# First norm's weights moved to the transposed rows, and the opening's queues written out by hand

## The chip, the cores and the metric

The kernel runs on one core of one Trainium2 chip. The metric is the device time of one execution in microseconds (us). Three executions of the kernel before took 1943.76, 1944.37 and 1944.44 us; the median is 1944.37 us.

## The reference

One layer is computed (DEPTH is 1) on 1024 tokens of width 1024 in float32: a feed-forward half step, an attention step and a second feed-forward half step. The change lies wholly in the first feed-forward step, and in what stands ahead of its first products:

```python
def rms_norm(x, gain):
    y = x * rsqrt(mean(x * x, axis=-1) + 1e-6)
    return y * gain

def swiglu(xn, w_in, w_out):          # w_in: 1024 x 5632, w_out: 2816 x 1024
    gate, up = split(xn @ w_in, 2)
    return (silu(gate) * up) @ w_out

x = x + 0.5 * swiglu(rms_norm(x, n1), wi1, wo1)      # n1 is g1 in the kernel
x = x + stick_breaking_attention(rms_norm(x, mix_norm), ...)
x = x + 0.5 * swiglu(rms_norm(x, n2), wi2, wo2)
```

## The kernel before, in words

**Three matmuls for one.** Each float32 operand is split into a high part, rounded to the matmul's own format by a copy on ACT, and a low part, which is the operand less its high part (`split`, L195: ACT at L197, the subtraction on DVE or POOL at L199). A product is then high by high, high by low and low by high, added up in PSUM (`mm3`, L347 to L349).

**The first feed-forward step.** The 2816 hidden columns are taken in 11 pairs of blocks of 128 (q = 0 to 10), gate and up. The rows of x are eight tiles of 128 tokens; the tokens of tiles 4 to 7 are the half T0, those of tiles 0 to 3 the half T1. Each row tile is normed (`norm`, L282), transposed on TensorE against an identity matrix (`turned`, L302, the transposes at L326, four into one PSUM bank), and split into `xh` and `xl`, which hold all of x transposed, eight blocks k of 128 features by 1024 tokens. Pair q = 0 is computed directly (`first_pair`, L433): four keys, (0,0), (1,0), (0,1) and (1,1), each a block of 128 hidden columns of gate (second number 0) or up (1); for each key and each half of the tokens 24 matmuls (8 blocks k by three). `FIRST[0]` (L64) gives the order of these, with the column ranges: 256 wide for as long as rows come in by pairs, 512 wide otherwise. The later pairs (`ffn_in`, L469) go by seven products instead of eight (`seven`, L532), which need sums of the quarters of x as well. These sums are the four tiles `tl`, which `turned` builds from the same PSUM banks (`mixes`, L310: copies on ACT, subtractions on DVE and one on POOL), and which `ffn_in` splits (L492) while the first pair runs on TensorE.

**The norm.** The sum of squares of a row tile is taken by halves of 512 features: one half on ACT (Square with a sum, L269), the other on DVE (L263). POOL adds the halves (L279), adds epsilon (L221) and raises to the power -0.5 (L222). DVE then scales the row by that rate and by the norm's weights in one instruction (L295). The weights vary along the row there, so they must stand in all 128 partitions: one row of 4 KB is loaded on ACT's queue (L230), spread over the partitions by two matmuls with a row of ones into two `ka` banks (L236), read from there for the first two rows and then copied to SBUF (L241), which frees the two banks.

**The opening.** SP's queue loads row tiles 4 and 5, the weights of gate for q = 0 (two transfers of 512 KB, runs of 1 KB), row tiles 6 and 7, the weights of up, row tiles 0 to 3 (`load_x`, `stream`, L748 to L752). TensorE runs 14 idle matmuls on zeros, before and between the first transposes (`WARM`, L70; L723). The first key runs on `mm3_late` (L352), which puts the matmuls with low parts last. Rows 6 and 7, then 0 and 1, then 2 and 3 are turned ahead of the steps (1,0), (1,2) and (4,0) of `FIRST[0]` (`turn_rows`, L733, and the table `at`, L775).

**What sets the order.** Each engine works through one queue in order. The program's scheduler fills the queues by priority, which is roughly the order of the program text; `following(mark)` puts an instruction behind the marked one on the same engine, without a wait for its end. Only some of the opening's instructions carry such a mark before.

Of the kernel before, what the change touches and what calls it, by code (L numbers as in the profile page):

```python
# [69 lines left out]
WARM = ((4, 3), (2, 1), (2, 2))  # L70
# [44 lines left out]
def macaron_kernel(ctx, tc, x, g1, w1_in, w1_out, gm, w_qkv, gq, gk, w_o, g2, w2_in, w2_out, out):  # L115
# [68 lines left out]
    above = cpool.tile([P, 96], F32, name="above")  # L184
# [10 lines left out]
    def split(raw, hi, lo, engine=None, after=(None, None)):  # L195
        with following(after[0]):
            first = act.activation(hi, raw, AF.Copy).ins  # L197
        with following(after[1]):
            return first, (engine or dve).tensor_tensor(lo, raw, hi.bitcast(F32), op=ALU.subtract).ins  # L199
# [17 lines left out]
    def root(pool, ss, inv_n):  # L217

        n = ss.shape[-1]
        a, y = (pool.tile([P, n], F32, name=f"rs_{i}", bufs=b) for i, b in (("a", 4), ("y", 2)))  # L220
        pool_e.tensor_scalar(a, ss, inv_n, EPS, op0=ALU.mult, op1=ALU.add)  # L221
        marks["root"] = pool_e.tensor_tensor(y, a, power.to_broadcast([P, n]), op=ALU.pow).ins  # L222
        return y

    HALVES = [slice(c * NHALF, (c + 1) * NHALF) for c in range(2)]

    def spread_gain(pl, g, ones):

        t = pl["xs"].tile([P, D], F32, name="gain", bufs=1)
        act.dma_start(t[0:1], g)  # L230
        spread = [bank("ka") for _ in HALVES]

        def put():
            for to, c in zip(spread, HALVES):
                with following(marks["warm"]):
                    marks["warm"] = pe.matmul(to, ones, t[0:1, c], start=True, stop=True).ins  # L236

        def keep(after):
            for src, c in zip(spread, HALVES):
                with following(after):  # L240
                    act.activation(t[:, c], src, AF.Copy)  # L241
            return [t[:, c] for c in HALVES]

        return spread, put, keep
# [10 lines left out]
    def squares(pl, row, tbs, ss, halves=(0, 1), shared=None, after=None):  # L255

        for i, tb in enumerate(tbs):
            for h in halves:
                to = ss[:, i, h : h + 1]
                if shared is not None and h:  # L260
                    x_ = row(tb, h)
                    with following(after and after[1]):
                        marks["squared"] = dve.scalar_tensor_tensor(  # L263
                            out=shared(i), in0=x_, scalar=1.0, in1=x_, op0=ALU.mult, op1=ALU.mult, accum_out=to
                        ).ins
                    continue
                junk = pl["hs"].tile([P, NHALF], F32, name="hs", bufs=1)
                with following(after and after[0]):
                    act.activation(junk, row(tb, h), AF.Square, accum_out=to)  # L269

    def rates(pl, row, tbs, ss=None, pooled=False, shared=None, after=None):

        n = len(tbs)
        if ss is None:
            ss = pl["xs"].tile([P, n, 2], F32, name="ss")
            squares(pl, row, tbs, ss, shared=shared, after=after)
        st = pl["xs"].tile([P, n], F32, name="st")
        with following(marks.get("root") if pooled else None):
            (pool_e if pooled else dve).tensor_tensor(st, ss[:, :, 0], ss[:, :, 1], op=ALU.add)  # L279
        return root(pl["xs"], st, 1.0 / D) if pooled else rsqrt(pl["xs"], st, 1.0 / D)  # L280

    def norm(pl, row, tbs, gain, ss=None, r=None, behind=None, pooled=False, shared=False, after=None):  # L282
# [4 lines left out]
        if r is None:  # L287
            to = [pl["xs"].tile([P, D], F32, name="xs") for _ in tbs] if shared else None
# [993 lines left out]
```

## Time and profile before

| | |
|---|---|
| median of 3 runs | 1944.37 us |
| the profiled execution's own time | 1945.78 us |
| its span, first to last instruction | 1943.9 us |
| granted TensorE clock, mean | 0.999 |
| TensorE (PE) busy | 1911.3 us, 98% of the span |
| VectorE (DVE), ScalarE (ACT), GpSimd (POOL) busy | 64%, 51%, 57% |
| first matmul of the first key (L360) starts at | 15.69 us |
| first matmul of pair q = 1 (L347, `ka`, 512 wide) starts at | 73.17 us |

The span is one execution on the chip. PE is TensorE's matmuls, PEld its weight loads, DVE is VectorE, ACT is ScalarE, POOL is GpSimd, SP the engine that issues most transfers. In a row of the timeline stand the start from the beginning of the span, the length, the engine, the line of the kernel, the operation, output <- inputs, the shape, the number of instructions merged, and in brackets the idle time ahead of it with what ended that. In a row of groups stand the count, the busy time in us, the mean of one in ns, and the idle time ahead. In a row of windows stand, for each engine, the busy time and the number of instructions, then the granted clock, the share of the DMA engines and the rate in GB/s.

### The profile page before, as it was taken

To read this page: it belongs to the slowest core of one execution; us is meant where nothing else is said; L and a number is where in the kernel's file an instruction comes from. 1 tells how busy PE (TensorE), PEld (TensorE's weight loads), DVE (VectorE), ACT (ScalarE), POOL (GpSimd) and SP (SyncE) were. 2 spreads that over 40 slices of the span, in tenths; PEclk is the share of its full clock that TensorE was granted. 3 is DMA by queue.
4 is the path that set the end of the run, shared out by engine and by line. 5 is a ranking of instruction groups with operands and counts; after the bars stand their busy time and mean duration, and the time that the engine had idled before them with its cause. 6 is when DMAs were issued, how large, how long until landed. Compare 5 with 4: busy or idle time off the path is not lost.

```text
span 1943.9 us, 26741 instructions
## 1 busy us (share of the span) xinstructions
PE 1911.3 (98%) x9410; PEld 1627.5 (84%) x9410; DVE 1246.6 (64%) x1711; ACT 984.0 (51%) x1796; POOL 1106.9 (57%) x993
## 2 busy tenths in 40 slices
PE   8999999999999999999999999999999999999999
PEld 7878888888888898898989897788888888888887
DVE  6855545544775757878787788477555545548545
ACT  5433343344335467777787877344433443343332
POOL 4566666755455746656655665114667666654554
PEclk9999999999999999999999999999999999999999
DMA  5233232337997411011011135521323232369983
GB/s 196 72 106 120 98 103 88 128 106 268 345 321 259 138 33 43 29 46 47 28 39 44 60 110 173 175 74 45 130 87 125 92 103 95 124 206 345 326 274 142
DMA packets 168361, 259.71 MB, mean 134 GB/s; under 512 B 11553, under 2 KB 81185, under 8 KB 168226
## 3 DMA queue, kind: packets, MB, share of 16 engines
q1 hardware_dynamic: 168224, 258.00, 39.1%
q8 instruction: 74, 1.21, 0.3%
q14 instruction: 61, 0.50, 0.1%
q10 hardware_dynamic: 2, 0.00, 0.0%
HBM read 197.66 MB, written 60.29 MB: 133 GB/s over the span
## 4 chain that ended last, share of the span: by engine, by line
PE 82%; DVE 9%; ACT 3%; POOL 2%; issue 2%; DMA 1%; SPq 0%; ACTq 0%; DVEq 0%; POOLq 0%
PE ka L347 6%; PE ka L348 6%; PE ka L349 6%; PE kc L347 4%; PE kc L348 4%; PE kc L349 4%; PE bq L347 4%; PE kb L347 4%; PE kb L348 4%; PE kb L349 4%; PE bq L348 4%; PE bq L349 3%; PE ma L349 3%; PE ma L348 3%; PE ma L347 3%; PE mb L348 3%
## 5 line engine op out<-in xcount | busy, mean ns | idle before, releaser
L199 POOL TENSOR_TENSOR rp<-raw,rp 128x1024 fp32r<-128x1024 f32 x84 | 209.0, 2493 | 173.0 <-ACT rp L197 157.7
L199 POOL TENSOR_TENSOR u<-sf,u 128x512 fp32r<-128x512 f32 x160 | 227.2, 1422 | 137.2 <-ACT u L197 137.2
L199 POOL TENSOR_TENSOR u<-raw,u 128x512 fp32r<-128x512 f32 x135 | 198.0, 1471 | 159.5 <-ACT u L197 158.5
L988 POOL TENSOR_TENSOR w<-w,om 128x512 f32<-128x512 f32 (+4 forms) x128 | 141.0, 1105 | 114.9 <-DVE om L981 88.6
L197 ACT ACTIVATE u<-sf 128x512 fp32r<-128x512 f32 x160 | 100.9, 631 | 204.3 <-PE kb L348 87.1
L485 DVE TENSOR_TENSOR h<-h 128x512 f32<-128x512 f32 x110 | 135.4, 1234 | 85.9 <-POOL h L589 85.1
L197 ACT ACTIVATE rp<-rh 128x1024 fp32r<-128x1024 f32 (+1 forms) x78 | 76.6, 985 | 202.1 <-issue 73.8
L347 PE MATMUL bq<-wqh,xh 128*128 128x384 f32 x512 | 174.7, 341 | 0.0
L349 PE MATMUL bq<-wqh,xl 128*128 128x384 f32 x512 | 172.2, 336 | 0.0
L348 PE MATMUL bq<-wql,xh 128*128 128x384 f32 x512 | 172.1, 336 | 0.0
L197 ACT ACTIVATE u<-raw 128x512 fp32r<-128x512 f32 x136 | 85.1, 632 | 152.4 <-PE ka L348 100.1
L611 DVE TENSOR_TENSOR raw<-raw 128x1024 f32<-128x1024 f32 (+1 forms) x60 | 91.6, 1529 | 104.6 <-DMA raw<-w_out 94.9
L348 PE MATMUL ka<-xl,u 128*128 128x512 f32 (+1 forms) x408 | 153.8, 377 | 2.8 <-DVE xl L199 2.8
L347 PE MATMUL ka<-xh,u 128*128 128x512 f32 (+1 forms) x408 | 153.8, 377 | 2.0 <-ACT s L537 1.7
L349 PE MATMUL ka<-xh,u 128*128 128x512 f32 (+1 forms) x408 | 153.5, 376 | 0.0
L349 PE MATMUL ma<-rp 128*128 128x512 f32 x352 | 137.1, 389 | 0.6 <-DVE rp L199 0.6
L347 PE MATMUL ma<-rp 128*128 128x512 f32 x352 | 137.0, 389 | 0.0
L348 PE MATMUL ma<-rp 128*128 128x512 f32 x352 | 136.9, 389 | 0.0
L589 POOL TENSOR_TENSOR h<-h,g 128x512 f32<-128x512 f32 x80 | 113.0, 1413 | 35.8 <-DVE h L541 34.0
L979 ACT ACTIVATE w<-bz,f 128x512 f32<-128x512 f32 (+2 forms) x192 | 112.5, 586 | 40.1 <-PE bz L975 39.1
L514 DVE TENSOR_TENSOR sf<-raw 128x512 f32<-128x512 f32 x80 | 78.2, 978 | 78.0 <-POOL u L199 78.0
L199 DVE TENSOR_TENSOR rp<-rh,rp 128x1024 fp32r<-128x1024 f32 (+1 forms) x70 | 109.6, 1583 | 24.6 <-ACT rp L197 20.0
(292 smaller groups left out, 5481.1 us busy)
## 6 DMA issues: line engine op xcount, KB each, us to landing
raw<-w_out SPq DMA_DIRECT2D x120, 512.0 KB, 5.5
raw<-w_in SPq DMA_DIRECT2D x88, 512.0 KB, 3.6
k<-h SPq DMA_DIRECT2D x154, 256.0 KB, 2.0
rh<-k SPq DMA_DIRECT2D x64, 512.0 KB, 5.9
raw_qkv<-w_qkv SPq DMA_DIRECT2D x64, 192.0 KB, 2.9
x_keep<-x SPq DMA_DIRECT2D x32, 256.0 KB, 3.7
x<-x_keep SPq DMA_DIRECT2D x32, 256.0 KB, 5.3
raw<-w_out SPq DMA_DIRECT2D x24, 256.0 KB, 3.5
```

Source lines behind the costliest of these rows:

```text
L197: first = act.activation(hi, raw, AF.Copy).ins
L199: return first, (engine or dve).tensor_tensor(lo, raw, hi.bitcast(F32), op=ALU.subtract).ins
L347: pe.matmul(dst, ah, bh, start=start and i == 0, stop=False, skip_group_check=onto)
L348: pe.matmul(dst, ah, bl, start=False, stop=False, skip_group_check=onto)
L349: last = pe.matmul(dst, al, bh, start=False, stop=stop and i == n - 1, skip_group_check=onto)
L485: dve.tensor_tensor(src, hb[of[0]], hb[of[1]], op=getattr(ALU, of[2]))
L514: dve.tensor_tensor(f[n], x, y, op=op)
L589: pool_e.tensor_tensor(h, h, gs[k], op=ALU.mult)
L611: dve.tensor_tensor(w[0], w[0], w[1], op=getattr(ALU, W_OF[m][2]))
L979: act.activation(to, z, AF.Sigmoid, scale=state["f", half][:, sign, tb % 4, hd : hd + 1])
L988: pool_e.tensor_tensor(wt[:, c1 : c0 + n], wt[:, c1 : c0 + n], om[:, c1 - 1 : c0 + n - 1], op=ALU.mult)
```

## The change

The norm's weights come in as 128 x 8 (`g1_sb`: feature block k in column k), so that after the transpose they are one number per partition. DVE scales a row by its rate alone, from SBUF to SBUF; the weights are applied where the transposed rows leave PSUM: by ACT as a scale with the high part, by DVE as a scale in the same instruction that subtracts the high part (`less`). The spread by matmuls, its two banks and its copies are gone.

Rows are turned in blocks: 4 and 5 (256 columns for each k), 6 and 7, then all four of 0 to 3, features 0 to 511 ahead of the last key of T0, features 512 to 1023 ahead of T1. So T1 runs 512 wide throughout. The copies of tiles 4 to 7 into `tl` are no longer made by ACT from PSUM, but by POOL as high plus low part (`whole_x`, two instructions of 4 x 256 for each pair of rows).

The first transfer of weights goes in pieces of 128 columns (runs of 512 bytes), so that both halves of the first key come ahead of the second key. The 14 idle matmuls become 13, all ahead of the first transposes. The power function is run once on a constant before it is needed. Nearly every instruction of the opening on ACT, DVE and POOL goes through `go`, which puts it behind the one before it on its engine in program order; so do the transposes and the first key on TensorE. The first work of pair q = 1 is put behind the last of these on each engine (`marks["open"]`).

```diff
 FIRST = (
-    ((0, 0, 256, (0, 1, 2)), (0, 256, 256, (0, 1, 2)), (0, 0, 512, (3,)),
-     (1, 0, 256, (0, 1)), (1, 256, 256, (0, 1)), (1, 0, 512, (2, 3))),
+    ((0, 0, 256, (0, 1, 2)), (0, 256, 256, (0, 1, 2)), (0, 0, 512, (3,)), (1, 0, 512, (0, 1, 2, 3))),
...
-WARM = ((4, 3), (2, 1), (2, 2))
+IDLE = 13
...
+    def go(engine, emit):
+
+        with following(marks.get(engine)):
+            marks[engine] = emit().ins
...
+    def mm3_late(dst, pairs, late):
+
+        n = len(pairs)
+        steps = []
+        for i in range(n + late):
+            if i < n:
+                steps.append((i, 0, 0))
+            if 0 < i <= n:
+                steps.append((i - 1, 0, 1))
+            if i >= late:
+                steps.append((i - late, 1, 0))
+        for i, (k, a, b) in enumerate(steps):
+            go("pe", lambda: pe.matmul(dst, pairs[k][0][a], pairs[k][1][b], start=i == 0, stop=i == len(steps) - 1))
...
-            with sooner(SOON if q == 1 else 0):
+            with sooner(SOON if q == 1 else 0), ExitStack() as held:
+                for mark in marks.pop("open", ()):
+                    held.enter_context(tc.issue_after(mark))
                 us = prepare(stream(pl, w_in, q, 0))
...
+                def square(tb, h, engine="act"):
+                    if tb not in xs:
+                        xs[tb] = pl["xs"].tile([P, D], F32, name="xs", bufs=4)
...
+                def scale(tb, h):
+                    go("dve", lambda: dve.tensor_scalar(
+                        xs[tb][:, HALVES[h]], rows_of[tb][:, HALVES[h]], r[:, tb : tb + 1], None, op0=ALU.mult
+                    ))
...
+                def high_x(tps, tbs):
+                    c = slice(tbs[0] * P, (tbs[-1] + 1) * P)
+                    for k, tp in tps.items():
+                        go("act", lambda: act.activation(xh[:, k, c], tp, AF.Copy, scale=g1_sb[:, k : k + 1]))
+
+                def less(out, tp, k, of):
+                    go("dve", lambda: dve.scalar_tensor_tensor(
+                        out=out, in0=tp, scalar=g1_sb[:, k : k + 1], in1=of, op0=ALU.mult, op1=ALU.subtract
+                    ))
...
+                def whole_x(tbs):
+                    c, q = slice(tbs[0] * P, (tbs[-1] + 1) * P), slice(tbs[0] % 4 * P, (tbs[-1] % 4 + 1) * P)
+                    for d, t in ((0, tl[0]), (1, tl[3])):
+                        go("pool", lambda: pool_e.tensor_tensor(
+                            t[:, :, q], xh[:, 4 * d : 4 * d + 4, c].bitcast(F32),
+                            xl[:, 4 * d : 4 * d + 4, c].bitcast(F32), op=ALU.add,
+                        ))
...
-                ahead = [stream(pr, w1_in, 0, 0)]
+                ahead = [stream(pr, w1_in, 0, 0, 2)]
...
+                for d in range(2):
+                    low(0, 1, d, "dve")
+                    for h in range(2):
+                        scale(6 + d, h)
+                behind = xs[7][:, D - 1 :]
+                for d in range(2):
+                    high(1, 1, d)
+                for d in range(2):
+                    low(1, 1, d, behind=None if d else behind)
+                square(0, 0)
+                square(0, 1)
+                square(1, 0)
+                square(1, 1, "dve")
+                rate(0, 2)
+                whole_x((4, 5))
+
+                def second_half():
+                    tps = turn_x((6, 7), range(KD))
+                    high_x(tps, (6, 7))
+                    low_x(tps, (6, 7))
+                    for tb in (2, 3):
+                        square(tb, 0)
+                        square(tb, 1, "dve")
+                    rate(2, 2)
+                    whole_x((6, 7))
+                    for tb in range(4):
+                        for h in range(2):
+                            scale(tb, h)
+                    marks["open"] = [marks[e] for e in ("act", "dve", "pool")]
+
+                def first_rows(d):
+                    tps = turn_x(range(4), range(4 * d, 4 * d + 4))
+                    high_x(tps, range(4))
+                    if d == 0:
+                        for k, tp in tps.items():
+                            go("act", lambda: act.activation(tl[2][:, k], tp, AF.Copy, scale=g1_sb[:, k : k + 1]))
+                    low_x(tps, range(4))
+                    for k, tp in tps.items():
+                        t1, t2, t3, t4 = (t[:, k % 4] for t in tl)
+                        if d == 0:
+                            less(t1, tp, k, t1)
+                        else:
+                            less(t3, tp, k, t3)
+                            less(t2, tp, k, t1)
+                            go("pool", lambda: pool_e.tensor_tensor(t4, t4, t2, op=ALU.subtract))
+
+                turns = {(1, 0): second_half, (2, 3): partial(first_rows, 0), (3, 0): partial(first_rows, 1)}
+                hb = first_pair(pa | pr, us, turns, FIRST[0], True)
```

`turn_x` transposes the given row tiles, feature block by feature block; `low_x` calls `less` for each block; `high` and `low` make the two parts of a block of weights; `rate` makes the rates of one or two row tiles on POOL; `square` takes half a row's sum of squares on ACT or DVE. The order of ACT's, DVE's and POOL's instructions is that of these calls.

More of the change, by code (lines that the diff above doesn't have):

```diff
@@ L193, in following, with split @@
         return tc.issue_after(mark) if mark is not None else nullcontext()
[L195 to L199, printed above, removed]
+    def split(raw, hi, lo, engine=None):
+        first = act.activation(hi, raw, AF.Copy).ins
+        return first, (engine or dve).tensor_tensor(lo, raw, hi.bitcast(F32), op=ALU.subtract).ins
     def rsqrt(pool, ss, inv_n, y=None):
@@ L221, in root @@
         pool_e.tensor_scalar(a, ss, inv_n, EPS, op0=ALU.mult, op1=ALU.add)
-        marks["root"] = pool_e.tensor_tensor(y, a, power.to_broadcast([P, n]), op=ALU.pow).ins
+        pool_e.tensor_tensor(y, a, power.to_broadcast([P, n]), op=ALU.pow)
         return y
     HALVES = [slice(c * NHALF, (c + 1) * NHALF) for c in range(2)]
[L227 to L244, printed above, removed]
     def load_gain(pl, g):
@@ L253, in rows, with squares, rates @@
         return slice(tb * P, (tb + 1) * P)
-    def squares(pl, row, tbs, ss, halves=(0, 1), shared=None, after=None):
+    def squares(pl, row, tbs, ss, halves=(0, 1)):
         for i, tb in enumerate(tbs):
             for h in halves:
[L259 to L266, printed above, removed]
                 junk = pl["hs"].tile([P, NHALF], F32, name="hs", bufs=1)
-                with following(after and after[0]):
-                    act.activation(junk, row(tb, h), AF.Square, accum_out=to)
-    def rates(pl, row, tbs, ss=None, pooled=False, shared=None, after=None):
+                act.activation(junk, row(tb, h), AF.Square, accum_out=ss[:, i, h : h + 1])
+    def rates(pl, row, tbs, ss=None, pooled=False):
         n = len(tbs)
@@ L454, in first_pair @@
                 ]
-                marks["key"] = (mm3_late if early and (n, i) == (0, 0) else mm3)(
-                    ps[t][key][:, c0 : c0 + width], pairs, after=marks.get("key") if early else None
-                )
+                to = ps[t][key][:, c0 : c0 + width]
+                if early:
+                    mm3_late(to, pairs, 4)
+                else:
+                    mm3(to, pairs)
             left[t] -= len(ks)
@@ L718, in macaron_kernel @@
+                go("pool", lambda: pool_e.tensor_tensor(r[:, :1], r[:, :1], power, op=ALU.pow))
                 idle = bank("kc")
-                def warm(n):
-                    for _ in range(n):
-                        with following(marks.get("warm")):
-                            marks["warm"] = pe.matmul(idle, zeros[:, :P], zeros, start=True, stop=True).ins
-                def normed(tbs, shared=False, after=None, behind=None):
-                    pending.extend(
-                        norm(
-                            pl, lambda tb, h: rows_of[tb][:, HALVES[h]], tbs, gain,
-                            pooled=True, shared=shared, after=after, behind=behind,
-                        )
-                    )
@@ L733, in turn_rows @@
-                def turn_rows(tbs):
-                    while pending:
-                        pending.pop(0)("kb", tl, after=marks["key"])
-                    if tbs:
-                        normed(tbs, behind=marks["turned"][1])
-                def weight(j, part, d, *args, **kwargs):
-                    us.setdefault((j, part), []).append(
-                        unit(pa | pr, columns(ahead[part][d], j), *args, **kwargs)
-                    )
-                warm(WARM[0][0])
-                gain, put_gain, keep_gain = spread_gain(pl, g1, ones)
@@ new lines, in macaron_kernel @@
+                for d in range(2):
+                    high(0, 0, d)
+                high(1, 0, 0, "dve")
+                tps = turn_x((4, 5), range(KD))
+                for d in range(2):
+                    low(0, 0, d, behind=None if d else behind)
+                high_x(tps, (4, 5))
+                low_x(tps, (4, 5))
+                high(1, 0, 1)
+                for d in range(2):
+                    low(1, 0, d)
+                for tb in (6, 7):
+                    square(tb, 0)
+                    square(tb, 1, "dve")
+                    rate(tb)
```

179 lines of the change are left out of this document (97 added, 82 removed).

## The prediction

> **What bounds the kernel now.** I read the page first, then TensorE's time in three stretches.
>
> ```profile
> span 1943.9 us, 26741 instructions
> PE 1911.3 (98%) x9410; PEld 1627.5 (84%) x9410; DVE 1246.6 (64%) x1711; ACT 984.0 (51%) x1796; POOL 1106.9 (57%) x993
> ```
> ```profile
> 0.00:73.17 73.17, 65.56 (x394) 0.98 0.39 134
> ...
> 140.00:1943.90 1803.90, 1780.54 (x8732) 1.00 0.40 134
> ```
>
> TensorE bounds the kernel. The change touches only what runs before 73.17, where pair q = 1 begins: what it gains or loses there moves everything behind it, unless the work behind it was not ready anyway. TensorE's waits up to 140 us, and its timeline:
>
> ```profile
> PE ka L348 <- DVE xl L199: 2.8, 3, 1.3
> PE ka L360 <- ACT gain L241: 1.7, 1, 1.7
> PE ka L347 <- ACT s L537: 1.7, 2, 1.5
> ...
> PE kb L326 <- ACT xh L197: 1.1, 1, 1.1
> PE ka L347 <- ACT xh L197: 0.4, 1, 0.4
> ```
> ```profile
> 15.69 1.22 PE L360 MATMUL ka<-xh,u 128*128 128x256 f32 x8 [1.74 <-ACT gain L241]
> ...
> 21.55 0.28 PE L347 MATMUL kc<-xh,u 128*128 128x256 f32 x1
> ...
> 24.43 1.52 PE L326 MATMUL kb<-ident,xs 128*128 128x128 f32 x12
> 27.00 0.63 PE L326 MATMUL kb<-ident,xs 128*128 128x128 f32 x4 [1.05 <-ACT xh L197]
> ...
> 28.70 0.39 PE L348 MATMUL ka<-xl,u 128*128 128x256 f32 x1 [0.96 <-DVE xl L199]
> ...
> 35.93 1.91 PE L326 MATMUL kb<-ident,xs 128*128 128x128 f32 x16
> 37.59 0.36 PE L347 MATMUL kc<-xh,u 128*128 128x256 f32 x1
> ...
> 40.55 0.40 PE L347 MATMUL kc<-xh,u 128*128 128x512 f32 x1
> ...
> 46.01 0.28 PE L347 MATMUL ka<-xh,u 128*128 128x256 f32 x1
> ...
> 73.17 0.39 PE L347 MATMUL ka<-xh,u 128*128 128x512 f32 x1
> ```
>
> From starts to starts: a key 256 wide takes 24.43 - 21.55 = 2.88, one 512 wide 46.01 - 40.55 = 5.46, 16 transposes 37.59 - 35.93 = 1.66. Between 15.69 and 73.17 lie 48 transposes, ten keys of 256 and three of 512: 5.0 + 28.8 + 16.4 = 50.2. The stretch is 57.5, so 7.3 are lost: the waits for `xh` and `xl` (4.3, and something at each restart), and the clock:
>
> ```profile
> 25.81:29.22 3.41, 1.40 (x11) 1.10 (x10) 3.41 (x6) 2.81 (x7) 1.99 (x4) 1.00 0.67 187
> 29.22:32.64 3.42, 3.42 (x18) 3.42 (x18) 2.72 (x5) 3.34 (x9) 0.32 (x2) 0.50 0.01 3
> ...
> 12.16:15.57 3.41, 1.78 (x12) 1.22 (x10) 2.81 (x4) 3.11 (x8) 2.15 (x2) 1.00 1.07 388
> ```
>
> After 3.41 us with TensorE busy for 1.40, the clock was 0.50 for 3.42: 1.7 us lost. After one with 1.78 busy it stayed at full.
>
> **The change, part by part.** The prices:
>
> ```profile
> 5.65 0.69 DVE L263 SCALAR_TENSOR_TENSOR xs<-x 128x512 f32<-128x512 f32 x1 [0.63 <-DMA x<-x]
> 5.73 1.04 POOL L222 TENSOR_TENSOR rs_y<-rs_a,power 128x1 f32<-128x1 f32 x1
> 6.80 2.74 DVE L295 SCALAR_TENSOR_TENSOR xs<-x,rs_y,ka 128x512 f32<-128x512 f32 x4 [0.45 <-POOL rs_y L222]
> ...
> 7.29 0.56 POOL L222 TENSOR_TENSOR rs_y<-rs_a,power 128x1 f32<-128x1 f32 x1
> ...
> 12.80 1.29 POOL L199 TENSOR_TENSOR u<-raw,u 128x512 fp32r<-128x512 f32 x1 [1.63 <-ACT u L197]
> 13.25 0.69 DVE L199 TENSOR_TENSOR xl<-kb,xh 128x512 fp32r<-128x512 f32 x1 [0.32 <-ACT xh L197]
> ...
> 15.05 1.07 ACT L241 ACTIVATE gain<-ka 128x512 f32<-128x512 f32 x2
> ...
> 19.92 6.38 POOL L199 TENSOR_TENSOR u<-raw,u 128x512 fp32r<-128x512 f32 x4
> 19.99 6.86 DVE L295 SCALAR_TENSOR_TENSOR xs<-x,rs_y,gain 128x512 f32<-128x512 f32 x4 [1.15 <-POOL rs_y L222]
> ...
> 58.43 0.68 DVE L318 TENSOR_TENSOR tl<-kb,tl 128x512 f32<-128x512 f32 x1
> ```
> ```profile
> L938 DVE SCALAR_TENSOR_TENSOR kl_s<-bz,gk_sb,kh_s 128x512 fp32r<-128x512 f32 x32 | 23.8, 743 | 13.7 <-ACT kh_s L937 13.6
> L1090 DVE COPY first<-ident 128x128 f32<-128x128 f32 x1 | 0.2, 220 | 0.0
> L937 ACT ACTIVATE kh_s<-bz,gk_sb 128x512 fp32r<-128x512 f32 x32 | 22.6, 706 | 8.4 <-PE bz L933 8.2
> L979 ACT ACTIVATE w<-bz,f 128x256 f32<-128x256 f32 x32 | 15.3, 479 | 11.0 <-PE bz L975 10.5
> L199 POOL TENSOR_TENSOR raw<-raw 128x1024 fp32r<-128x1024 f32 x2 | 4.8, 2395 | 0.2
> ```
> ```profile
> 19.50:24.00 4.50, 1.00 1.09 348
> 14.20:18.20 4.00, 1.00 1.02 409
> 641.75:643.00 1.25, 1.00 0.94 273
> ```
>
> *DVE beside POOL.* Four scalings (L295) took 2.74 alone, 0.69 each; beside POOL's subtractions four took 6.86, 1.72 each, and POOL's 1.6 instead of 1.29: they take turns. The subtraction from PSUM kept its 0.69 while POOL ran (13.25). So instructions with one input in PSUM, `less` among them, run freely; those from SBUF alternate with POOL, one for one.
>
> *Start.* Row 5 arrives at 5.65. Its square takes 0.7, its rate 0.3 + 0.56 (the first power, 1.04, is now run early): 7.3. Two scalings without weights: a copy of 128 took 0.22; for 512 I take 0.4, paced 0.34. So rows 4 and 5 are scaled by 8.05; before, the four scalings ended at 6.80 + 2.74 = 9.54. Sixteen transposes end at 9.5 and the first key can begin at 9.6, not 15.69, since the copies that free the `ka` banks (15.05, until 16.1) are gone. It then runs at the pace of `less`: 256 wide I take 0.4 each (half of L938's elements), ACT 0.36 (L979's 0.48 less overlap). The eight low parts start behind the second high part and DVE's copy of a weight block, at 9.9, and end at 13.2; the key ends at 13.8. If TensorE is still at half clock there, the key ends up to 2 us later, and nothing below moves by more than 0.2, because the third turn waits for DVE and POOL.
>
> *Edits that cost or bring nothing.* An idle matmul is a 512-wide one, 5.46 / 24 = 0.23 at full clock, 0.46 at half: 13 of them end by 8, before the first transposes, and TensorE has nothing else to do there. The weights in 128 short runs instead of one row are needed at 8.6; the row was there by 6.8 (L295 waited for POOL alone). The `tl` copies that ACT loses lay in its idle time, and POOL's new sums lie ahead of idle time, except where they meet the scalings (below). T1 all 512 wide saves 4 x 2.88 - 2 x 5.46 = 0.6, which is in the sum.
>
> *Weights in halves.* Whole rows (4 KB runs) came at 409 GB/s, runs of 1 KB at 348, runs of 512 bytes (the qkv weights) at 273: the 1 MB takes 3.8 us instead of 3.0, and what comes behind is 0.8 later. Row 5 in at 5.65, then 3.8, 2.6 for rows 6 and 7, 3.0 for the weights of up: all of these are there by 15.1 to 15.6. The 0.8 is covered: without it the third turn would come 0.02 earlier by the queues below. Were the loads 1.5 later still, the end would be 1.4 later.
>
> *Second and third key, second turn.* 13.8 + 2 x 2.88 = 19.5. ACT has the high parts of the last weights at 16.2; DVE's subtraction (0.69) and row 7's two scalings follow: 17.7. The turn ends at 21.2, and 0.3 is waited for the first low part (before: 2.0 and the half clock). Three keys end at 30.3.
>
> *Third turn.* It needs all of rows 0 to 3 scaled in their first halves, so row 3's rate and the queues ahead of it. POOL: low parts of key (1,1) from 18.0 (behind row 7's scaling), two of 1.29 and a DVE square between, to 21.1; rates of rows 0 and 1 to 22.4, `whole_x` of rows 4 and 5, two of 2.4. Between these DVE puts its square of row 2, waiting its turn, so that they end at 27.6; row 3's square ends at 28.2, the rates of 2 and 3 at 29.5. Then POOL begins `whole_x` of rows 6 and 7 at the moment at which DVE wants to scale rows 2 and 3: scaling, 2.4, scaling, 2.4, and row 3's first half is there at 35.1. TensorE, ready at 30.3, waits 4.8; the turn ends at 36.5.
>
> The price that decides is whether the scaling, with one tensor from SBUF, alternates with POOL. The ends are L295 (1.72 for 0.69) and the subtraction from PSUM (no loss); I take L295, the same job on the same rows. The Trainium skill, "SBUF — State Buffer", Who interferes with whom, says that the pair of ports that DVE shares with POOL is locked for a whole instruction, and names a scaling by a scalar among those that take it; by that the wait is as I put it, and no run here shows it for this instruction.
>
> *Key (1,1) and fourth turn.* Behind the third turn ACT makes four high parts and `tl` copies (L937's 0.71, paced 0.59): DVE's eight `less` start at 38.6 and end at 44.0 (0.67 each). Their banks are those of the fourth turn, so it ends at 44.5 and not 36.5 + 5.46 + 1.66 = 43.6. T1 takes 4 x 5.46 = 21.8: 66.4. The clock: a 4.8 us wait leaves some 3.41 us with under 1.4 busy, so 3.4 us at half cost 1.7, of which the 0.9 before the fourth turn hides a part: +0.9. The first pair ends at **67.3 instead of 73.17, 5.9 earlier**. The Trainium skill, "TensorE: Matmul & The Clock Gate", Part 1 (The HAM clock gate), asks for a whole idle window before the clock falls; the trace had it fall after one 41% busy, and the measurement decides. By the page the end could be 66.4.
>
> *Behind it.* Pair q = 1 needs DVE's sums. Before, the last sum (58.43 + 0.6) led the end of the first pair by 14.1, and TensorE still waited 0.2 and 1.5 in q = 1 (L537 in the list of waits). After: DVE's 22 instructions from 38.6 (eight, two products, four, eight) end at 53.1, a lead of 14.2. So these waits stay, and 5.9 reaches the end. The first sums of q = 1 may now be queued right behind the scalings (`marks["open"]`), ahead of the third turn's `less`: two of 0.69 to 1.72, hidden as long as DVE waits there for ACT (35.4 to 38.6), else up to 0.2 late.
>
> The sum: span 1943.9 - 5.9 = 1938.0; that execution, 1945.78 with 1.9 around its span, becomes 1939.9. The median of the runs is 1.4 below it: **1938.5**.
>
> **Rivals.** *The scaling does not alternate with POOL.* Then row 3 is scaled by 30.7, the third turn waits 0.5, and the first pair ends at 61.9: 11.3 saved, 1933.1. For it: the scaling has one tensor input. Against it: L295's rows.
>
> *DVE gives most of it back.* The scaling keeps L295's 0.69 and alternates: row 3 is there at 38.8, the first pair ends at 70.0, with the clock 71.2: 2.0 saved, 1942.4. For it: the row is the only one of this shape. A DVE chain that falls behind TensorE in q = 1 would come out alike.
>
> *The order is not what the text says.* The later keys carry no mark, so the scheduler may put key (1,1) ahead of the third turn. It then fills the wait, but the fourth turn loses its cover: third turn 35.8 to 37.4, low parts to 45, end of the pair 67 to 68.5: about 1939.5.
>
> *Slower: the clock stays at half behind the third turn.* Each 3.41 us window at half costs 1.7. From the fourth it eats the gain, from the sixth the kernel is slower by over 0.2%; through key (1,1) and T1 (29 us of work) it is 27 more, some 1966. For it: the fourth turn comes in drops, so windows may again be too empty. Against it: before, one full window brought the clock back, and T1 is 21.8 us without a gap.
>
> **Numbers.** Forecast 0.45 (alone 1936.5 to 1941), free scaling 0.22, most given back 0.18, other order 0.08, slower 0.07. The range takes in the free scaling and the given-back case: 1933.0 to 1943.5, which leaves out the slow case and tails, some 0.15. About 0.2% (3.9 us) is what a measurement of this kernel can tell from no change, so faster means under 1940.5: 0.40 of the forecast, all of the free scaling, most of the other order: 0.67. Same: the rest of the forecast and the given-back case, 0.26. Slower: 0.07.
>
> **What would show it.** Right: first key near 9.6; no wait over 0.5 at the second turn; a wait of 3 to 5 us for `xs` at the third, with `whole_x` on POOL between the scalings of rows 2 and 3; clock 0.50 for one window behind it; q = 1 at 66 to 68; the rest as long as before. Wrong: no wait there (free scaling), a first key behind 12, or new waits in q = 1.

## The result, and the profile after

The changed kernel takes 1953.65 us (median of 5, 1951.96 to 1955.82) beside 1944.44 for the kernel before in the same rounds (1943.76 to 1945.02): the ratio is 1.0047, 95% interval 1.0032 to 1.0061. It is 9.2 us slower; 5.9 less was forecast. The profiled execution took 1954.04, its span 1952.3.

TensorE's timeline answers to the steps of the opening:

```profile
8.81 3.43 PE L743 MATMUL kb<-ident,xs 128*128 128x128 f32 x15 [1.27 <-DVE xs L714]
11.93 0.55 PE L324 MATMUL ka<-xh,u 128*128 128x256 f32 x2
...
20.71 1.91 PE L743 MATMUL kb<-ident,xs 128*128 128x128 f32 x16
...
35.39 0.33 PE L743 MATMUL kb<-ident,xs 128*128 128x128 f32 x1 [2.83 <-DVE xs L714]
39.27 3.04 PE L743 MATMUL kb<-ident,xs 128*128 128x128 f32 x13 [3.56 <-DVE xs L714]
41.96 1.09 PE L324 MATMUL kc<-xh,u 128*128 128x512 f32 x2
...
47.90 1.91 PE L743 MATMUL kb<-ident,xs 128*128 128x128 f32 x16
49.57 0.71 PE L324 MATMUL ka<-xh,u 128*128 128x512 f32 x2
...
71.45 0.39 PE L308 MATMUL ka<-xh,u 128*128 128x512 f32 x1
```

The order is the forecast one: first key, second turn, third turn with its wait, key (1,1), fourth turn, T1. But the first key starts at 11.93 instead of 9.6, the third turn ends at 42.0 instead of 36.5, and pair q = 1 begins at 71.45: 1.7 ahead of the kernel before (73.17), 4.2 behind the forecast. So the opening did get shorter, and everything that made the kernel slower lies behind it. TensorE's waits, and its three stretches (the granted clock stands third from the end):

```profile
PE kb L743 <- DVE xs L714: 8.3, 4, 3.6
...
PE bz L1046 <- DVE w L1052: 4.0, 7, 1.7
PE ka L308 <- ACT s L498: 3.5, 3, 2.4
PE ma L308 <- DVE h L502: 2.7, 1, 2.7
```
```profile
0.00:71.45 71.45, 61.49 (x342) 54.07 (x342) 54.28 (x82) 36.66 (x70) 45.69 (x45) 0.93 0.43 144
71.45:140.00 68.55, 65.11 (x278) 52.76 (x277) 46.00 (x50) 28.34 (x50) 48.39 (x33) 0.98 0.34 111
140.00:1952.30 1812.30, 1784.20 (x8741) 1519.59 (x8739) 1149.64 (x1595) 912.76 (x1669) 1028.59 (x920) 1.00 0.39 133
```

The clock was 0.93 in the opening, where it was 0.98. Set against the waits of before, three have grown or are new beside the one in the opening: `s` in q = 1 (3.5, was 1.7), `ma` at the last product of the first step (2.7, was none; 0.6 stood there for `rp`), `bz` in the attention step (4.0, was 1.5). Two of them also let the clock fall. Laying the same matmuls of the two traces side by side, the changed kernel stands 1.7 ahead at 71.45, 1.9 behind at 132, 6.9 behind at 466, 9.8 behind at 1002, 8.4 behind at the end. Between these points 3.6, 5.0 and 2.9 are lost, and 1.4 comes back behind 1002, which no run here looked into. The three losses one by one:

*In q = 1.* POOL, DVE and ACT behind the fourth turn:

```profile
58.06 9.30 POOL L846 TENSOR_TENSOR tl<-tl,tl 128x512 f32<-128x512 f32 x1
```
```profile
58.04 2.35 DVE L197 TENSOR_TENSOR t0l<-tl,t0h 128x1024 fp32r<-128x1024 f32 x2
60.30 1.22 DVE L197 TENSOR_TENSOR t1l<-tl,t1h 128x1024 fp32r<-128x1024 f32 x1
...
66.21 0.69 DVE L426 TENSOR_TENSOR h<-kc,h 128x512 f32<-128x512 f32 x1
```
```profile
68.64 1.06 ACT L196 ACTIVATE t3h<-tl 128x1024 fp32r<-128x1024 f32 x1 [8.47 <-POOL tl L846]
69.60 0.58 ACT L425 ACTIVATE h<-ka 128x512 f32<-128x512 f32 x1
70.08 1.14 ACT L196 ACTIVATE u<-sf 128x512 fp32r<-128x512 f32 x2
```

The other three of POOL's four subtractions took 1.3 each. This one lasted 9.30, from 58.06 to 67.36, and DVE's unbroken row of instructions with SBUF inputs ended at 66.2. ACT's last part of t3 waits 8.5 for it, and the weights of q = 1 (`u`) stand behind that in ACT's queue: the first `sf` weights come at 70.1, in the kernel before at 65.4:

```profile
65.36 0.63 ACT L197 ACTIVATE u<-sf 128x512 fp32r<-128x512 f32 x1 [1.45 <-DVE sf L514]
```

By 87 TensorE has waited off 1.2 of its lead of 1.7.

*The clock.* Windows of TensorE around two waits, at the third turn and near 125 (the first busy time is TensorE's):

```profile
32.54:35.96 3.42, 0.34 (x2) 0.14 (x1) 3.20 (x3) 0.00 (x0) 3.42 (x3) 1.00 0.00 0
35.96:39.37 3.41, 0.10 (x1) 0.10 (x2) 3.41 (x3) 0.00 (x0) 2.97 (x2) 0.50 0.00 0
39.37:42.79 3.42, 3.42 (x15) 3.32 (x16) 0.84 (x2) 2.50 (x4) 0.00 (x0) 0.50 0.23 81
...
124.70:128.10 3.40, 1.04 (x5) 0.67 (x4) 1.51 (x3) 2.15 (x4) 1.23 (x1) 1.00 0.04 16
128.10:131.50 3.40, 3.40 (x9) 2.63 (x8) 2.35 (x2) 0.63 (x1) 1.30 (x2) 0.50 0.25 62
```

The wait for `s` near 125 was 1.5 before and is 2.4 now: TensorE comes to it 0.6 earlier than before, and ACT 0.3 later. The lead alone does not explain it. In e1, e2 and e3 (next section) TensorE comes to it at three other times, in e3 1.8 earlier than in the changed kernel, and waits the same 2.4. ACT's `s` hangs there on DVE's queue (just ahead of it in ACT's queue one instruction waited 5.67 for `g` from DVE), and DVE lost time near 85, in two sums of weights. Here is the first of them, in the changed kernel and in the kernel before:

```profile
84.74 1.78 DVE L475 TENSOR_TENSOR sf<-raw 128x512 f32<-128x512 f32 x1
```
```profile
85.28 0.68 DVE L514 TENSOR_TENSOR sf<-raw 128x512 f32<-128x512 f32 x1
```

In the changed kernel the two took turns with POOL (1.78 and 1.58); in the kernel before they ran free (0.68 and 0.69). Over all 14 traces this goes with the wait: it is 1.5 in the three in which the two sums ran free (before, f7, i2), and 1.8 to 2.4 in the eleven in which they took turns. No run changed these two sums alone. At 1.5 the window stayed busy enough (1.95 of 3.41 before); at 2.4 it was busy for 1.04 of 3.40, and the next one ran at half, which cost 1.6 more.

*At the product with `w_out`, the last of the first feed-forward step, and in the attention step:*

```profile
462.93 0.79 PE L308 MATMUL ma<-rp 128*128 128x512 f32 x1 [2.69 <-DVE h L502]
```
```profile
924.74 0.47 ACT L1050 ACTIVATE w<-bz,f 128x256 f32<-128x256 f32 x1 [2.00 <-DMA o_keeph<-w]
```

Neither line is touched by the change, and from 90 us on the instructions of TensorE, DVE, ACT and POOL stand in the same order in both traces, by their tiles and shapes. What the change moved there is told by the experiments.

### The profile page after: what moved, and what is told of

Same layout as the page of the kernel before. It is cut to its first block, busy times and chain, and to the rows that moved or that the text cites. A ratio compares the mean times of both kernels' runs of the same rounds, so it can differ in the third digit from the quotient of the medians.

```text
span 1952.3 us, 26654 instructions
## 1 busy us (share of the span) xinstructions
PE 1910.8 (98%) x9357; PEld 1626.4 (83%) x9357; DVE 1249.9 (64%) x1727; ACT 977.8 (50%) x1787; POOL 1122.7 (58%) x997
## 4 chain that ended last, share of the span: by engine, by line
PE 84%; DVE 7%; POOL 3%; ACT 3%; issue 2%; DMA 1%; DVEq 0%; SPq 0%; ACTq 0%; POOLq 0%
PE ka L308 6%; PE ka L309 6%; PE ka L310 6%; PE kc L310 4%; PE kc L308 4%; PE kc L309 4%; PE ma L308 4%; PE ma L309 4%; PE ma L310 4%; PE bq L308 4%; PE bq L309 4%; PE bq L310 4%; PE kb L310 3%; PE kb L308 3%; PE kb L309 3%; PE bo L1099 3%
## 5 line engine op out<-in xcount | busy, mean ns | idle before, releaser
L197 POOL TENSOR_TENSOR u<-raw,u 128x512 fp32r<-128x512 f32 x128 | 183.8, 1438 | 159.5 <-ACT u L196 158.8
L574 DVE TENSOR_TENSOR raw<-raw 128x1024 f32<-128x1024 f32 (+1 forms) x60 | 87.4, 1459 | 113.2 <-DMA raw<-w_out 96.9
L196 ACT ACTIVATE u<-raw 128x512 fp32r<-128x512 f32 x128 | 80.3, 631 | 150.6 <-PE ka L309 100.8
L308 PE MATMUL ka<-xh,u 128*128 128x512 f32 x352 | 138.0, 392 | 3.5 <-ACT s L498 3.5
L309 PE MATMUL ka<-xl,u 128*128 128x512 f32 x352 | 137.6, 391 | 0.0
L310 PE MATMUL ka<-xh,u 128*128 128x512 f32 x352 | 137.5, 391 | 0.0
```

The source lines that it names most:

```text
L308: pe.matmul(dst, ah, bh, start=start and i == 0, stop=False, skip_group_check=onto)
L309: pe.matmul(dst, ah, bl, start=False, stop=False, skip_group_check=onto)
L310: pe.matmul(dst, al, bh, start=False, stop=stop and i == n - 1, skip_group_check=onto)
L574: dve.tensor_tensor(w[0], w[0], w[1], op=getattr(ALU, W_OF[m][2]))
```

## The experiments

All times are medians; "before" in each row is the kernel before in the same rounds. "q = 1" is the start of its first matmul in the profiled execution.

| run | edit | us | before | ratio, 95% interval | q = 1 |
|---|---|---|---|---|---|
| changed | | 1953.65 | 1944.44 | 1.0047, 1.0032 to 1.0061 | 71.45 |
| e1 | old bank places | 1949.71 | 1944.55 | 1.0025, 1.0013 to 1.0036 | 71.94 |
| e2 | sums behind scalings | 1944.95 | 1944.55 | 1.0006, 0.9997 to 1.0015 | 66.20 |
| e3 | last sums on DVE | 1951.05 | 1944.55 | 1.0036, 1.0024 to 1.0049 | 71.31 |
| e4 | e1, e2 (all sums) and e3 | 1939.94 | 1944.55 | 0.9976, 0.9967 to 0.9985 | 62.82 |
| f1 | 51 short matmuls at the start | 1955.35 | 1943.95 | 1.0065, 1.0051 to 1.0079 | 78.99 |
| f3 | first weights whole | 1952.15 | 1943.95 | 1.004, 1.0027 to 1.0052 | 72.49 |
| f7 | kernel before, new bank places | 1947.19 | 1943.95 | 1.0016, 1.0007 to 1.0025 | 72.97 |
| g1 | e4, 8 wide and 37 short idle | 1937.82 | 1943.95 | 0.9975, 0.9966 to 0.9984 | 68.28 |
| h1 | e4, 45 idle of 144 columns | 1938.39 | 1945.25 | 0.9967, 0.9955 to 0.998 | 66.13 |
| h2 | e4, 64 idle of 104 columns | 1943.28 | 1945.25 | 0.9993, 0.9985 to 1.0002 | 70.30 |
| i1 | 51 short matmuls in the gap | 1952.76 | 1944.41 | 1.0039, 1.0025 to 1.0052 | 72.70 |
| i2 | 26 wide matmuls in the gap | 1947.39 | 1944.41 | 1.0014, 1.0005 to 1.0023 | 70.89 |

**e1 and f7: the places of the banks.** A bank gets its place in PSUM when its name is first drawn. Before, the two `ka` banks of the spread were drawn ahead of the first `kb`; the change took the spread out, so `kb` came first and all places moved.

```diff
                 idle = bank("kc")
+                for _ in range(2):
+                    bank("ka")
```

> The changed kernel, with two more PSUM banks drawn ahead of the first transposes, so that the banks get the places that they had before the change; no instruction is added. Theory: the wait of 2.7 us at the start of the last product of the first step (ma behind DVE's last h) comes from the place of one bank: ma's third bank lies where the last product of pair q = 10 is still read. Then this wait goes, and with it the 3.4 us at half clock behind it: 4.3 to 4.6 us less, about 1949.2. Rival: DVE's chain is late there by itself; then the wait stays and the time is that of the changed kernel, 1953.6.

Measured: 1949.71, 3.9 less, near the 1949.2 expected. TensorE's timeline in e1 has no wait there, and its clock stays at full there:

```profile
459.02 0.39 PE L310 MATMUL kb<-t3h,u 128*128 128x512 f32 x1
459.25 0.39 PE L308 MATMUL ma<-rp 128*128 128x512 f32 x1
```

f7 makes the same move alone, in the kernel before (`for _ in range(4): bank("kb")` behind its `idle`).

> The kernel before, with only the order changed in which its PSUM banks are first drawn (the four kb banks ahead of ka's two, as in the changed kernel); same instructions in the same order. Theory: this alone brings the wait of 2.5 to 3 us at the start of the first step's last product, and where the clock falls behind it 1.6 more: 1947 to 1949. Rival: without the change the wait does not arise, 1944.4.

Measured: 1947.19, 3.2 more, within the expected range, and f7's list of waits has the row, with DVE's last `h` as releaser:

```profile
PE ma L347 <- DVE h L541: 2.7, 1, 2.7
```

So the place of one bank, and nothing of the norm, costs 2.7, and 1.6 more where the clock falls behind it (in f7, f1 and f3 it did not). `ma`'s third bank then lies on the `kb` bank that the last product of q = 10 filled, which DVE reads last of all.

**e2: what makes the third turn wait.** POOL's `whole_x((6, 7))` is emitted behind the scalings, and an instruction of one column that reads row 3's last scaled column makes POOL wait for them:

```diff
-                    whole_x((6, 7))
                     for tb in range(4):
                         for h in range(2):
                             scale(tb, h)
+                    last = xs[3][:, D - 1 :]
+                    go("pool", lambda: pool_e.tensor_tensor(tl[0][:, 0, 256:257], last, last, op=ALU.mult))
+                    whole_x((6, 7))
```

> The changed kernel, with POOL's two sums of rows 6 and 7 (whole_x) made to wait until DVE has scaled rows 0 to 3. Theory: the third turn waits because DVE's scalings of rows 2 and 3 take turns with these sums, three waits of 2.5, 2.5 and 1.5 us; row 3 is then scaled by 34 to 34.5 instead of 39.2, the wait for xs at the third turn falls from 6.4 to 2 or 2.5, and the first pair ends at 65.5 to 67 instead of 71.45; if everything behind it moves along, the kernel takes 1947.5 to 1949.5. First rival: DVE's scalings are slow there whatever POOL does; nothing changes. Second rival: the sums of pair q = 1 are late for another reason than the turn, and TensorE waits the gain off there: the first pair ends early, q = 1's waits grow by as much, and the time stays within 1 us of 1953.6.

Measured: 1944.95, 8.7 less, below the expected range (the changed kernel's own rows of the same place stand first, DVE and POOL, then DVE in e2):

```profile
25.36 2.76 DVE L699 SCALAR_TENSOR_TENSOR xs<-x 128x512 f32<-128x512 f32 x1
...
28.05 2.88 DVE L699 SCALAR_TENSOR_TENSOR xs<-x 128x512 f32<-128x512 f32 x1
...
30.87 1.70 DVE L714 TENSOR_SCALAR xs<-x,r 128x512 f32<-128x512 f32 x4
32.78 6.83 DVE L714 TENSOR_SCALAR xs<-x,r 128x512 f32<-128x512 f32 x4 [0.22 <-POOL r L711]
```
```profile
25.17 5.21 POOL L766 TENSOR_TENSOR tl<-xh,xl 128x1024 f32<-128x1024 f32 x2
...
32.72 4.82 POOL L766 TENSOR_TENSOR tl<-xh,xl 128x1024 f32<-128x1024 f32 x2
37.49 1.44 POOL L197 TENSOR_TENSOR u<-raw,u 128x512 fp32r<-128x512 f32 x1
```
```profile
32.74 1.68 DVE L714 TENSOR_SCALAR xs<-x,r 128x512 f32<-128x512 f32 x4 [0.61 <-POOL r L711]
```

Four scalings take 1.68 without POOL and 6.83 beside it: the forecast's mechanism, now shown. Row 3 is there at 34.0, and q = 1 begins 5.25 earlier. By the medians that gain was kept. How much more than it was gained is not settled: e2 spreads widely, from 1942.28 to 1950.19, and the profiled execution was its longest, 3.9 below that of the changed kernel.

**e3: POOL's last sums.** The subtraction t4 less t2 goes to DVE:

```diff
-                            go("pool", lambda: pool_e.tensor_tensor(t4, t4, t2, op=ALU.subtract))
+                            go("dve", lambda: dve.tensor_tensor(t4, t4, t2, op=ALU.subtract))
```

> The changed kernel, with the last four subtractions of the opening (t4 less t2) on DVE instead of POOL. Theory: one of them stood on POOL for 9.3 us, shut out by DVE's unbroken row of instructions, and ACT's last part of t3 and all weights of q = 1 stood behind it in ACT's queue; on DVE they cost four times 0.7, t3's last high part comes by 65 instead of 68.6, the waits for s in q = 1 (3.5 in all, longest 2.4) fall below 1.7, the clock stays at full at 128, and the kernel is 3 to 4 us faster: 1949.6 to 1950.7. Rival: POOL's long row tells nothing, or DVE's 2.8 us more of work take the place of it: within 0.7 us of 1953.6.

Measured: 1951.05, 2.6 less. ACT's timeline (one row) and the list of waits in e3:

```profile
65.70 1.04 ACT L196 ACTIVATE t3h<-tl 128x1024 fp32r<-128x1024 f32 x1
```
```profile
PE ka L308 <- ACT s L498: 2.6, 2, 2.4
```

t3's last part comes 2.9 earlier, and TensorE, 0.1 ahead of the changed kernel at 71, is 1.7 ahead from 87 to 128. That much of the theory holds. The wait of 2.4 near 125 stayed, against the theory, as the two sums of DVE near 85 took turns here too (1.78 and 1.60). That the clock did not fall behind it was the place of the windows in this execution: the wait was spread over two, busy for 2.09 and 2.38. The time is just above the expected range, and the runs overlap the changed kernel's (1950.2 to 1952.86 beside 1951.96 to 1955.82), so the 2.6 is less sure than what the trace shows.

**e4: all three.** e1 and e3 as above; all four sums stand behind the scalings, first tile 0 of `tl` for both pairs of rows, then tile 3.

> The three edits of the other runs together, and all four of POOL's sums (those of rows 4 and 5 too) behind the scalings, those of features 0 to 511 first. Theory: DVE's squares of rows 1 to 3 no longer take turns either; row 3 is scaled by 31.5 to 33, the wait at the third turn is under 1.5, the clock stays at full, q = 1 begins at 64 to 66, its waits are under 2, the wait at the last product is gone: 1937 to 1941, faster than the kernel before (1944.4). Rival, what is gained ahead of q = 1 is waited off in it: 1943 to 1946.

Measured: 1939.94, 4.6 less than the kernel before and within the expected range. There is no wait at the third turn, q = 1 begins at 62.82, 10.4 ahead of before. Of that, 6.5 arrives in the span (1937.4): the wait of 1.8 near 116 costs a window of the clock, which was expected to stay at full, and the attention step's `bz` waits 3.6.

**f1, i1: the program's own loads.** The page's DMA queues, and the DMA view of the changed kernel from 919 to 926, where the two stores of one block are on their way (the last row is one of them, with its size and the time from issue to landing):

```profile
q8 instruction: 73, 1.20, 0.3%
```
```profile
q1 hardware_dynamic: 288, 0.52, 20.4%
q8 instruction: 1, 0.02, 1.3%
o_keeph<-w SPq DMA_DIRECT2D x1, 256.0 KB, 3.9
```

73 loads of 16 KB are 1.20 MB; over TensorE's 9357 matmuls and as many weight loads that is 64 bytes each, so by the size these are pieces of TensorE's program, 256 instructions a piece. One falls on the stores at 920.7, which land after 3.9 instead of 2.0, and one on those at 988.1 (4.3). In the kernel before, the same stores took 2.0 with no load beside them. The change takes 51 matmuls out of the opening (53 rows of the trace, where the two of the spread stand as four) and so moves every later load against the work. f1 gives them back as short ones behind the idle ones:

```diff
+                for _ in range(51):
+                    go("pe", lambda: pe.matmul(idle[:, :16], zeros[:, :P], zeros[:, :16], start=True, stop=True))
```

> The changed kernel with 51 short idle matmuls (128x16) behind its 13 idle ones, so that TensorE runs as many instructions as before the change. Theory: two stores in the attention step (o_keeph, 920.7 and 988.1 in the changed kernel) took 3.9 and 4.3 us to land instead of 2.0, and TensorE waited for them (bz behind w, 4.0 in all instead of 1.5), because loads of TensorE's own program (16 KB each, one for each stretch of instructions) fell upon them; the change took 51 matmuls out of that program and so moved every later load by some 10 us against the work. With the count restored all o_keeph stores up to 1125 take 2.0, the bz wait is 1.5 to 2, and the kernel is 2 to 2.8 us faster, 1951 to 1951.6. The first turn comes up to 3 us later, which the wait at the third turn hides. Rival: the stores are late because two more DMAs are issued (weights in halves), or by chance; then they stay at 3.5 to 4.5 or move elsewhere, and the time stays at 1953.6.

Measured: every store up to 1125 takes 2.0, and the waits for `w` fall from 4.0 to 1.3; yet the time is 1955.35. The theory of the stores holds, and over all 14 traces: these two stores took 3.5 to 4.6, with one load of the program on each, in the six with 9357 matmuls (the changed kernel, e1 to e4, f3), and 2.0, with none, in the other eight. But the short matmuls spoiled the start: q = 1 begins 7.5 later (the clock in f1 is shown in the last section). i1 puts them into the third turn's gap, on a `ka` bank.

> The changed kernel with the 51 short idle matmuls (128x16) not ahead of the first turn, where they kept the clock at half and made the start 7.5 late, but ahead of the third turn, where TensorE waits 6.4 us anyway. At 0.11 each at full clock they take 5.5 of it. Theory: the start stays as it is, row 3 is scaled at 39.2 as before, so the first pair still ends at 71.5 to 72.5; the o_keeph stores all take 2.0, bz waits 1.3 to 1.5 instead of 4.0, and the end is 2 to 2.7 us earlier: 1951 to 1951.7. Rival: the loads of the program had no part in it; 1953.6.

```profile
PE bz L1050 <- DVE w L1056: 1.5, 8, 0.3
```

Stores again 2.0, `bz` 1.5, and in i1's trace 2.7 of its lag goes between 665 and 994. The median is only 0.9 less, within the spread of the runs and above the expected range: at half clock the 51 take 8.4 instead of 5.5, and the third turn comes 0.9 late.

**f3: weights whole.** `stream(pr, w1_in, 0, 0)` without the 2.

> The changed kernel with the first weights in whole transfers, as before the change. As forecast, halves neither cost nor bring anything at the end, since the third turn waits for DVE and POOL: within 1 us of 1953.6, with the first key's second half not later than DVE needs it. Rival: the two transfers that go restore the stores of the attention step to 2.0 and the bz waits to 1.5: 2 to 2.8 us less.

Measured: 1952.15, 1.5 less instead of at most 1, with runs of 1949.16 to 1954.5 that overlap the changed kernel's. With whole weights the opening is 1.0 longer, and the lead that is then missing would have been waited off anyway: the halves decide nothing at the end that these runs can tell. The stores stay late (4.2 and 4.0), so the two transfers had no part in that.

**i2: wide matmuls in the gap.** The same place, 26 of 512 columns.

> The changed kernel with 26 idle matmuls of 512 columns ahead of the third turn (6 us at 0.23 each, in the wait of 6.4). Theory: columns keep the clock up, so the third turn's last 13 transposes take 1.4 instead of 3.0 and the half clock of 7 to 10 us there is gone or one window long: the first pair ends at 69.5 to 70.5 instead of 71.45 to 71.9. What of it reaches the end is open: q = 1's chain hangs on POOL and DVE, so by the theory that it gives the opening's gains back, less than 1 us, beside the 2 to 2.7 us of the stores, which these 26 instructions also move: 1950 to 1951.5. Rival: the gain of the clock reaches the end in full: 1948 to 1950.

Measured: 1947.39, 6.3 less, below the expected range and below the rival's. TensorE, its windows and POOL in i2:

```profile
32.14 6.09 PE L836 MATMUL ka<-xl 128*128 128x512 f32 x26
38.06 0.49 PE L743 MATMUL kb<-ident,xs 128*128 128x128 f32 x3
39.71 1.64 PE L743 MATMUL kb<-ident,xs 128*128 128x128 f32 x13 [1.16 <-DVE xs L714]
```
```profile
33.05:36.46 3.41, 3.41 (x16) 2.81 (x15) 3.34 (x2) 0.00 (x0) 3.41 (x3) 1.00 0.03 5
36.46:39.87 3.41, 2.25 (x12) 1.67 (x11) 3.41 (x3) 0.00 (x0) 2.92 (x2) 1.00 0.00 0
```

```profile
56.14 5.76 POOL L850 TENSOR_TENSOR tl<-tl,tl 128x512 f32<-128x512 f32 x3
```

The last 13 transposes take 1.64 instead of 3.04, and the third turn ends 0.8 earlier. What was not expected: POOL's subtractions took turns with DVE here, 2.28 and 2.27 instead of 9.30, though the order is the changed kernel's. Laid beside the changed kernel's matmuls, i2 stands 0.6 earlier at 71, 1.5 at 87 (ACT's queue is no longer held up), 2.4 at 127 (the two sums near 85 run free, and the wait near 125 is 1.5 again), 4.0 at 132 (the clock stays at full), 3.5 at 665 and 6.0 at 994 (the stores are at 2.0). So of the 6.2 between the two spans 0.6 is the opening, 0.9 and 0.9 lie in q = 1, 1.6 is a window of the clock, and 2.6 the program's loads, less 0.5 of drift between 132 and 665.

**g1, h1, h2: e4 with the loads moved.** g1: 8 idle matmuls of 512 columns and 37 of 16. h1, h2: 45 of 144, 64 of 104 in place of the 13.

> The kernel of the three edits together, with 8 idle matmuls of 512 and 37 of 16 columns instead of 13 of 512, which moves the loads of TensorE's program off the stores of the attention step. Theory: the stores take 2.0, the bz wait falls from 3.6 to 1.5 or 2, the first turn begins no later than 9.3 and its end is not moved: 1937 to 1938.5 against 1939.9. Rival: the stores are late for another reason; 1939.9.

> The kernel of the three edits with 45 idle matmuls of 144 columns instead of 13 of 512: nearly as many columns, so as much work for TensorE and the clock, but 32 instructions more, which brings the loads of its program about 5 us earlier against the attention step. Theory: at full clock 144 columns take 0.11 us and hide the weight load; they end by 8.5, ahead of the second row, the first pair ends at 62.5 to 63.5 as in the run of the three edits, the o_keeph stores at about 906 and 973 take 2.0, the bz wait falls from 3.6 to 1.5: 2 us less than 1939.9, 1937 to 1938.5. Rival: another store is met instead; a wait for w of 1 to 2 us elsewhere, 1939 to 1940.

> The same with 64 idle matmuls of 104 columns, which gives TensorE as many instructions as the kernel before had. Theory: all o_keeph stores up to 1110 take 2.0 and the bz wait is 1.5; but at half clock each takes 0.2 for its weight load, so that they end by 10 to 10.5 and the first turn is 1 to 1.5 late, of which q = 1's own chain hides a part: 1937 to 1939. Rival: columns keep the clock up and they end by 9: 1936.5 to 1937.5.

In all three the stores take 2.0 and `bz` waits 1.5; in all three the start suffers, most in h2, because the idle matmuls ran on at half clock. TensorE in h1:

```profile
1.64 9.88 PE L690 MATMUL kc<-xl 128*128 128x144 f32 x45 [1.64 <-POOL xl L683]
```

45 in 9.88 are 0.22 each, where full clock was expected to give 0.11. g1 (1937.82) and h1 (1938.39) lie in their expected ranges and are faster than the kernel before, like e4; h2 (1943.28) is 4.3 above its range and can't be told from the kernel before. That g1 is better than e4 is not shown: its ratio is 0.9975, e4's 0.9976.

## Why the prediction was wrong, step by step

- *Start.* Forecast 9.6, measured 11.93. The rows were scaled by 9.15 instead of 8.05 (POOL's mean of row 5 took 0.66 beside DVE's scalings of row 4), and the 15 transposes ran at half clock, 3.43 instead of 1.7. That this would not move the end held: the third turn waited anyway.
- *Third turn.* The mechanism was right, the size wrong. The wait of 4.8 was 6.4, and row 3 came at 39.2 instead of 35.1. Mis-sized terms: both squares of DVE, not one, took turns with POOL's sums (2.76 and 2.88), so that the rates came at 32.7, not 29.5; and the first low part of q = 1 (37.49, 1.44), which I had put behind the scalings, took a turn too.
- *Clock.* 0.50 for two windows (6.83), where one was forecast; the turn's last 13 transposes alone lost 1.6.
- *From the third turn's end to the end of the first pair.* Forecast 30.8 with the clock, measured 29.5. Close.
- *"So these waits stay, and 5.9 reaches the end."* This is the step that failed, and with the next one it turned the sign, for the opening itself was still 1.7 shorter. I followed DVE's queue and found its lead unchanged; that held nearly (its last sum of the opening ends 13.3 ahead of q = 1, forecast 14.2). But all four of POOL's subtractions now lie behind the fourth turn, two of them no longer in idle time near 41 to 45, and one was shut out for 9.3; ACT's queue hung on it: 1.2 lost by 87. Then the longer wait near 125 cost 0.9 and a window of the clock 1.6, which makes 3.6 between 71 and 132. e3 and i2 each bring back 1.6 to 1.8 of the waits and the clock's 1.6.
- *"The rest as long as before."* The forecast put this at nothing, without a reason. Behind 132 lie 4.4 from the place of one bank with its window, 0.5 of drift (e1: 3.9 less, f7: 3.2 more), and some 2.7 from the program's loads on two pairs of stores (i1 2.7, i2 2.6).
- *The whole.* The forecast span was 1938.0, the measured one 1952.3. Of these 14.3, 4.2 are the opening, 3.6 the way to 132, 5.0 that to 466 and 2.9 that to 1002; 1.4 came back.
- *Edits at nothing.* Halves of weights: nothing that can be told at the end (f3). T1 at 512: as forecast, four keys from 49.57 to 71.45, 21.9 against 21.8.
- *Rivals.* "Most given back" named a chain that falls behind TensorE in q = 1, which came, through POOL. Free scaling and the other order did not; nor did a clock that stays down. The other order could not come: in the changed kernel all keys of the first pair go through `mm3_late` and `go` (264 matmuls at L324). The description of the change says so of the first key alone, and this rival rests on that. That the kernel could be slower through things that the change does not mean to touch was no rival of mine.

On the page "SBUF — State Buffer" of the Trainium skill, Who interferes with whom: whoever issues first holds the shared ports for a whole instruction. The scalings agree (e2). It says nothing of an instruction shut out across nine of the other engine, as at 58.06, where waiting for one instruction was all that the rule gave reason to expect.

## What to carry to other kernels

An edit in the opening changes the order in which banks are first drawn and the length of TensorE's program; compare the waits of all later instructions before and after, and count what that costs, before taking "the rest stays" for granted. Follow every queue to its last instruction, POOL's too: the engine that ends the chain was not the one that I had followed. Whether two sums met POOL or missed it went, in all traces, with the length of a wait 40 us later. A wait that leaves a window of 3.41 less than half busy can cost another 1.7.

## What the runs showed of the hardware

- **Where the clock falls.** Most windows with TensorE busy for 1.74 of 3.41 or less were followed by one at half (1.03 and 1.04 in the changed kernel, 1.74 in e2 at 31.29); after 1.79 (e4 at 4.96) and 2.25 (i2) it stayed at full. These traces show no sharp limit: it also stayed at full after 1.55 (f3 at 458.11) and 1.57 (f1 at 464.62).
- **The windows do not start with the kernel.** The changed kernel and e1 run the same opening; the gap at the third turn cost one 6.83 at half, the other 10.24. The page "TensorE: Matmul & The Clock Gate" of the Trainium skill, Part 1 (The HAM clock gate), calls the window free-running, and the traces agree. The times of the kernels with this gap spread widely, the changed one over 3.9 and e2 over 7.9 (1942.28 to 1950.19); those of the kernel before over 1.3 in the same rounds as the changed one. In e2 the clock goes with the time: the mean granted clock was 0.997 in the four slowest runs and 1.000 in the four fastest.
- **Short matmuls don't hold the clock.** In f1, with TensorE recorded as busy throughout (51 matmuls of 16 columns, then transposes), the clock fell and stayed down:

```profile
7.22:10.64 3.42, 3.42 (x32) 3.37 (x31) 1.60 (x4) 1.03 (x2) 2.26 (x4) 1.00 1.13 350
10.64:14.05 3.41, 3.41 (x18) 3.41 (x17) 0.00 (x0) 0.00 (x0) 2.74 (x3) 0.50 1.06 361
```

  144 and 104 columns (h1, h2) did not bring it up either, for as long as they ran; 13 of 512 columns did (the changed kernel, at full from 5.24), and 26 held it (i2). What the gate counts is not what the profile calls busy.
- **POOL shut out.** The subtraction of 9.30 lasts 9.27 to 9.30 in six traces (the changed kernel, e1, e2, f1, f3, i1). In each, DVE's first instruction on SBUF begins 0.02 to 0.05 ahead of it (58.04 and 58.06 above), and eight more follow without a gap. In i2, DVE's first begins at 56.88, in the middle of POOL's 56.14, and the two take turns from there. So the two traces of one order differ by how the row of DVE met POOL's; which rule lets POOL in or not, the runs don't tell.
